# The first weight block of a seven-product pair behind plain or down columns is split one column sooner

## Chip, core and metric

The kernel runs on one core of one Trainium2 chip. The metric is the device time of one execution in microseconds (us). Engines are called as the profile calls them: PE multiplies matrices (PEld is its weight load), DVE, ACT and POOL work on elements, SP issues most DMAs.

## What is computed

One layer of a decoder, for a prompt of 512 tokens and for 32 sample tokens (8 sequences of 4) with the same weights; the kernel holds all 544 tokens side by side. Cut to what matters here:

```python
D_MODEL = 1024
D_FF = 2816

def _swiglu(x, w_gate, w_up, w_down):
    return (jax.nn.silu(x @ w_gate) * (x @ w_up)) @ w_down

def _layer(x, pos, p, attn_cache, ml_state):
    x = x + 0.5 * _swiglu(_rmsnorm(x, p['ffn1_norm']), p['ffn1_w_gate'], p['ffn1_w_up'], p['ffn1_w_down'])
    h = _rmsnorm(x, p['mix_norm'])
    ...
    x = x + mix @ p['w_out']
    x = x + 0.5 * _swiglu(_rmsnorm(x, p['ffn2_norm']), p['ffn2_w_gate'], p['ffn2_w_up'], p['ffn2_w_down'])
```

Between the two lines, `h` is projected by `w_in`, and dilated attention and mLSTM heads make `mix` from it. Everything is float32. The two SwiGLU blocks (ffn1 and ffn2) are the parts that the change touches.

## The kernel before

**Split operands.** A float32 product is made of three faster ones. Each operand is split into a high part (a rounded copy, made on ACT) and a low part (what is left, a subtraction on DVE). PE then adds high x high, high x low, low x high. For the weights the parts are the tiles `whi` and `wlo`. Both come, like the temporary `ws`, from one rotation of eight buffers (tag `wsp`): a new tile takes the buffer of the one eight before it and waits until that one has been read.

**Columns.** PE works column by column, one column being 128 columns of a weight matrix. `run` gets a list of jobs. A plain `Job` is one column: 8 blocks of 128 rows, each with 3 products for 2 halves of the tokens, 48 matmuls. A down column (a `Job` on `w_down`) is of the same kind; its result is added to the residual `xT[m]` by one DVE instruction, `x<-mm,x`. In the first plain columns of a block the gate and up results also pass through DVE and ACT (`zg`, `zu`, `hh`, `hl`), and `FastNorm.operands` prepares the sums of activation blocks that the pairs need (`xn`, `xd`, split into `oh` and `ol`).

**Seven-product pairs.** A `Fast` job computes two gate and two up columns together, as a product of 2x2 blocks with seven block products where the plain way has eight. The activation sides of the seven are `b11`, `t1`, `t2`, `b22`, `t3`, `b21` and `t4`, all prepared before. Each of the seven steps is 24 matmuls. Its weight side is made by `Fast.split(n)`:

- step 0: the raw block `a11`, split;
- step 1: `ws = a21 + a22`, split; step 2: `ws = ws - a11`, split; step 3: `ws = a12 - ws`, split (one tile, overwritten each time);
- step 4: `a21 = a11 - a21` in the raw tile (`wraw<-wraw` in the profile), split; steps 5 and 6: `a12` and `a22`, split.

So steps 1 to 4 cost two DVE instructions and one on ACT. The products accumulate in PSUM: steps 0, 2, 4 and 6 in one bank pair (`a`), steps 1 and 3 in two smaller ones (`c`, `aux` in the profile), step 5 in another. After steps 0, 1 and 2 ACT copies the bank as it stands (`p1`, `p5`, `p6`, all `p` in the profile): the next step into the same bank may start only after its copy.

**Raw blocks.** The raw tiles (`wraw`) have three buffers. The loader starts the DMAs of a raw tile when the one three before it is used up; for a pair that is at step 4 for the upper half (`top`) and step 6 for the lower (`low`).

**What sets the order.** The order of instructions on each engine is fixed while the program is built. `Order` keeps a clock for each engine and a list of threads (generators). A thread yields a time, and maybe a condition, at which it may go on. `poll` lets threads go on whose time has come by PE's clock; it is called after each block of rows (6 matmuls in a column, 3 in a pair). Threads with a lower priority number go first. `cost` holds the planned durations: on DVE 0.15 us + 1.05 ns for each element of a row, on ACT for a copy 0.18 us + 0.75 ns, on PE one matmul of 272 in 272 / 2180 us. A thread that waits for a result yields mostly the planned end + 0.2 - 0.3 us. These times decide only which instruction is written first; on the chip each engine takes its instructions in the order written and waits for semaphores.

**The splitter.** In `run`, one thread goes through the jobs in order and writes the splits. `pos[n]` is the place of job n in units, a plain job counting 2 and a pair 7, and `unit[0]` is where PE is: it is set when a column begins and grows by one with each step of a pair. A plain job is split when PE has reached `pos[n] - 4` (`pos[n] - 3` behind a pair). Step s of a pair is split when PE has reached `pos[n] + s - 2`, step 1 at `pos[n] - 2`.

A block of 2816 hidden columns is done in three parts (8, 8 and 6 blocks of 128). In each half the first part has 8 plain columns, 2 pairs and 8 down columns; the second 4 pairs and 8 down columns; the third 3 pairs and 8 down columns. So there are six places at which a pair follows a plain or a down column: one behind plain and two behind down columns in each half. Between the halves lies the mixing stage (attention and mLSTM), in which all engines work.

Of the kernel before, what the change touches and what calls it, by code (L numbers as in the profile page):

```python
# [52 lines left out]
class Order:  # L53
# [89 lines left out]
    def R(self, *aps):  # L143
        return max(self.ready.get(a.tensor.name, (0.0, ""))[0] for a in aps) + 0.2

    def U(self, *aps):
        return max(self.used.get(a.tensor.name, (0.0, ""))[0] for a in aps) + 0.2
# [100 lines left out]
def hybrid_layer_kernel(ctx: ExitStack, tc: tile.TileContext, I: dict, C: dict, O: list):  # L248
# [20 lines left out]
    def aux():  # L269
        return pax.tile([P, 512], F32, name="aux", tag="aux")  # L270
# [16 lines left out]
    def mm(out, lhsT, rhs, start=True, stop=True, beside=False, **kw):  # L287
        nc.tensor.matmul(out, lhsT, rhs, start=start, stop=stop, **kw)  # L288
        n = size(rhs)
        od.issue("pe", 0.05 if beside else n / (2180.0 if rhs.dtype == F32R else 595.0), [out], [lhsT, rhs],  # L290
                 False, (part(lhsT.shape[0]), part(size(lhsT))))
# [314 lines left out]
    at, unit, used = [0], [0], [0]  # L606

    def run(jobs):
        raws = []
        pos, n = [], 0  # L610
        for j in jobs:
            for r in (j.top, j.low) if isinstance(j, Fast) else (j.raw,):
                if r not in raws:
                    raws.append(r)
            pos.append(n)
            n += 7 if isinstance(j, Fast) else 2

        def loader():
            for n, r in enumerate(raws):
                if n >= 3:  # L620
                    old = raws[n - 3]
                    yield 0, 0, lambda: old.left == 0
                    yield U(old.t)
                if r.t is None:
                    r.load()
            yield 0

        def splitter():
            for n, j in enumerate(jobs):
                if isinstance(j, Fast):  # L630
                    for s in range(7):
                        raw = j.low if s else j.top
                        yield 0, 0, lambda: unit[0] >= pos[n] + s - (3 if s == 1 else 2) and raw.t is not None
                        yield from j.split(s)
                else:
                    ahead = 3 if n and isinstance(jobs[n - 1], Fast) else 4
                    yield 0, 0, lambda: unit[0] >= pos[n] - ahead and j.raw.t is not None
                    yield R(j.raw.t) - 0.3
                    yield from j.split()

        od.spawn(loader(), 0)
        od.spawn(splitter(), 1)
        od.poll()

        def slot():
            od.need(lambda: od.avail("mm", 1))
            od.take("mm", 1)
            ps = pmm.tile([P, 2, 512], F32, name="mm", tag="mm")
            od.poll()
            return ps  # L650

        def products(j, ps, ks, hs=(0, 1)):
            od.need(lambda: j.w is not None)
            hi, lo = j.w
            for k in ks:
                od.need(lambda: j.xs(k) is not None)
                xh, xl = j.xs(k)
                for a, (w, x) in enumerate(((hi, xh), (hi, xl), (lo, xh))):
                    for h in hs:
                        mm(ps[:, h, :HN], w[:, k, :], x[:, h * HN:(h + 1) * HN],  # L660
                           start=j.start and k == 0 and a == 0, stop=j.stop and k == j.nk - 1 and a == 2)
                od.poll()

        def finish(j, ps):
            if j.stop:
                od.spawn(j.after(ps[:, :, :HN], ps), 0)
                od.poll()

        kept = [None]

        def fast(j, more):
            bank = {"a": kept[0] or slot()}
            for n, (name, b) in enumerate(j.steps):
                unit[0] += n > 0
                od.need(lambda: j.w[n] is not None)
                hi, lo = j.w[n]
                if n == 1:
                    od.need(lambda: sum(f <= od.t for f in od.free["aux"]) >= 2)
                    od.take("aux", 2)
                    bank["c"] = aux(), aux()  # L680
                elif n == 5:
                    bank["b"] = slot()
                for i in range(2):
                    ps = bank[b][i] if b == "c" else bank[b][:, i]
                    for k in range(4):
                        od.need(lambda: j.op(name, k) is not None)
                        xh, xl = j.op(name, k)
                        for a, (w, x) in enumerate(((hi, xh), (hi, xl), (lo, xh))):
                            mm(ps[:, :HN], w[:, 4 * i + k, :], x, start=n in (0, 1, 5) and k == 0 and a == 0,
                               stop=k == 3 and a == 2, skip_group_check=True)  # L690
                        od.poll()
                od.spawn(j.post(n, bank, more), 0)
                od.poll()
            kept[0] = bank["b"] if more else None

        first = [(j, slot()) for j in jobs[:2]]
        for ks in (range(0, 4), range(4, 8)):
            for i, (j, ps) in enumerate(first):
                for k in ks:
                    products(j, ps, (k,))  # L700
                    used[0] = max(used[0], k + 1)
                    od.poll()
                if 7 in ks:
                    finish(j, ps)
                    at[0], unit[0] = i + 1, pos[i + 1]
        for i, j in enumerate(jobs[2:]):
            at[0], unit[0] = i + 2, pos[i + 2]
            if isinstance(j, Fast):
                fast(j, isinstance(jobs[i + 3], Fast))
                continue  # L710
            if j.start:
                ps = slot()
            if j is jobs[-1]:
                for h in range(2):
                    products(j, ps, range(j.nk), (h,))
                    od.spawn(last_half(h, ps[:, h, :HN]), 0)
                    od.poll()
                continue
            products(j, ps, range(j.nk))
            finish(j, ps)  # L720
# [133 lines left out]
    jobs = ffn_jobs("ffn1", lambda: n1, n2.add)  # L854
# [976 lines left out]
    def last_half(h, ps):  # L1831
        m = KD - 1
        x = xT[m]
        h_ = slice(h * HN, (h + 1) * HN)
        dve.scalar_tensor_tensor(x[:, h_], ps, 0.5, x[:, h_], op0=OP.mult, op1=OP.add)
        yield R(x), 1
        p = aux()
        yt = t2("yt", (P, 2, P))
        if h:
            yst = t2("yst", (NS, P))  # L1840
            tr(p[0:NS, 2 * P:3 * P], x[:, S:N], ident)
        for b in range(2):
            c = (2 * h + b) * P
            tr(p[:, b * P:(b + 1) * P], x[:, c:c + P], ident)
        if h:
            dve.tensor_copy(yst, p[0:NS, 2 * P:3 * P])
        act.copy(yt.rearrange("p b d -> p (b d)"), p[:, 0:2 * P])
        done(p)
        yield R(yt) - 0.3
        if h:  # L1850
            dma.dma_start(ysm[:, m * P:(m + 1) * P], yst)
        dma.dma_start(yp[:, 2 * h:2 * h + 2, m * P:(m + 1) * P], yt)
# [96 lines left out]
```

## Time and profile before

| | us |
|---|---|
| median of 3 runs | 1116.19 |
| lowest, highest | 1116.14, 1116.45 |
| profiled execution | 1116.02 |
| its span, first to last instruction | 1114.2 |

The profile is of one execution. Times in it count from the span's start. A row of the timeline gives the start, the duration, the engine, the line of the kernel (226 and 288 are lines of helpers that write all element work and all matmuls), the operation, output<-inputs, shapes and, in brackets, how long the engine was idle before it and for whom. Matmuls are drawn with a modelled length (0.29 us for 272 columns), although the next one starts 0.125 us after: their starts count, not their ends. A row of the waits gives who waited for whom, the total in us, how often, and the longest. A row of the stretches gives the length, then busy time and count of PE, PEld, DVE, ACT and POOL, the granted clock, the DMA engines' share and GB/s.

### The profile page before, as it was taken

To read this page: it belongs to the slowest core of one execution; us is meant where nothing else is said; L and a number is where in the kernel's file an instruction comes from. 1 tells how busy PE (TensorE), PEld (TensorE's weight loads), DVE (VectorE), ACT (ScalarE), POOL (GpSimd) and SP (SyncE) were. 2 spreads that over 40 slices of the span, in tenths; PEclk is the share of its full clock that TensorE was granted. 3 is DMA by queue.
4 is the path that set the end of the run, shared out by engine and by line. 5 is a ranking of instruction groups with operands and counts; after the bars stand their busy time and mean duration, and the time that the engine had idled before them with its cause. 6 is when DMAs were issued, how large, how long until landed. Compare 5 with 4: busy or idle time off the path is not lost.

```text
span 1114.2 us, 21328 instructions
## 1 busy us (share of the span) xinstructions
PE 1095.4 (98%) x8807; PEld 1043.7 (94%) x8807; DVE 750.6 (67%) x1178; ACT 507.9 (46%) x926; POOL 94.1 (8%) x104
## 2 busy tenths in 40 slices
PE   7999999999999999999999999999999999999998
PEld 5999999999999999998887977999999999999997
DVE  5888338873487779678776746688862788537852
ACT  5545215551255455466744544453541355314541
POOL 0000000000000000174444310000000000000000
PEclk9999999999999999999999999999999999999999
DMA  7214412342134547684987494341242222422232
GB/s 234 79 39 132 126 48 77 111 155 76 39 95 132 169 148 168 192 247 125 308 271 252 158 320 155 104 131 56 76 151 76 77 76 76 152 77 76 67 108 58
DMA packets 143404, 145.36 MB, mean 130 GB/s; under 512 B 9028, under 2 KB 120964, under 8 KB 143308
## 3 DMA queue, kind: packets, MB, share of 16 engines
q1 hardware_dynamic: 143244, 144.01, 41.8%
q8 instruction: 69, 1.13, 0.4%
q14 instruction: 27, 0.22, 0.1%
q0 software_dynamic: 64, 0.00, 0.0%
HBM read 132.57 MB, written 9.18 MB: 127 GB/s over the span
## 4 chain that ended last, share of the span: by engine, by line
PE 89%; DVE 6%; ACT 2%; issue 1%; DMA 1%; SPq 0%; DVEq 0%; ACTq 0%
PE mm L288 73%; PE aux L288 13%; PE aux L294 4%; DVE wlo L226 2%; ACT whi L226 2%; DVE ws L226 1%; DVE wraw L226 1%; DMA wraw<-in_ffn_w_up_dram 1%; DMA xt<-in_x_prompt_dram 0%; DVE zu L226 0%; DVE ol L226 0%; ACT p L226 0%; DVE xd L226 0%; SPq L226 0%; DVE hl L226 0%
## 5 line engine op out<-in xcount | busy, mean ns | idle before, releaser
L226 ACT CAST whi<-wraw 128x1024 fp32r<-128x1024 f32 (+3 forms) x180 | 174.2, 988 | 130.5 <-PE mm L288 97.2
L226 DVE TENSOR_TENSOR wlo<-wraw,whi 128x1024 fp32r<-128x1024 f32 (+3 forms) x180 | 208.2, 1165 | 22.8 <-ACT whi L226 22.7
L288 PE MATMUL mm<-oh,wlo 128*128 128x272 f32 x720 | 209.6, 291 | 2.1 <-DVE wlo L226 2.0
L288 PE MATMUL mm<-oh,whi 128*128 128x272 f32 x720 | 207.5, 288 | 0.0
L288 PE MATMUL mm<-ol,whi 128*128 128x272 f32 x720 | 207.2, 288 | 0.0
L288 PE MATMUL mm<-xh,whi 128*128 128x272 f32 x704 | 153.7, 300 | 0.2 <-ACT whi L226 0.2
L288 PE MATMUL mm<-hh,whi 128*128 128x272 f32 x704 | 147.3, 289 | 0.5 <-DVE x L226 0.5
L288 PE MATMUL mm<-xl,whi 128*128 128x272 f32 x704 | 146.0, 289 | 0.5 <-DVE xl L226 0.5
L288 PE MATMUL mm<-hl,whi 128*128 128x272 f32 x704 | 146.5, 288 | 0.0
L288 PE MATMUL mm<-hh,wlo 128*128 128x272 f32 x704 | 146.4, 288 | 0.0
L288 PE MATMUL mm<-xh,wlo 128*128 128x272 f32 x704 | 146.0, 289 | 0.3 <-DVE wlo L226 0.3
L288 PEld LDWEIGHTS mm<-oh,wlo 128*128 128x128 f32 x720 | 135.5, 188 | 5.4 <-DVE wlo L226 4.4
L226 DVE SCALAR_TENSOR_TENSOR x<-mm,x 128x544 f32<-128x544 f32 (+1 forms) x49 | 34.9, 713 | 154.9 <-PE mm L288 154.9
L288 PEld LDWEIGHTS mm<-oh,whi 128*128 128x128 f32 x720 | 135.6, 188 | 0.0
L288 PEld LDWEIGHTS mm<-ol,whi 128*128 128x128 f32 x720 | 135.5, 188 | 0.0
L288 PEld LDWEIGHTS mm<-xh,whi 128*128 128x128 f32 x704 | 109.8, 189 | 12.3 <-issue 11.6
L288 PEld LDWEIGHTS mm<-hh,whi 128*128 128x128 f32 x704 | 110.8, 188 | 0.9 <-DVE x L226 0.7
L288 PEld LDWEIGHTS mm<-xl,whi 128*128 128x128 f32 x704 | 110.7, 189 | 0.8 <-DVE xl L226 0.8
L288 PEld LDWEIGHTS mm<-xh,wlo 128*128 128x128 f32 x704 | 110.8, 189 | 0.6 <-DVE wlo L226 0.6
L288 PEld LDWEIGHTS mm<-hh,wlo 128*128 128x128 f32 x704 | 110.9, 188 | 0.0
L288 PEld LDWEIGHTS mm<-hl,whi 128*128 128x128 f32 x704 | 110.7, 188 | 0.0
L226 ACT CAST whi<-ws 128x1024 fp32r<-128x1024 f32 x54 | 56.7, 1051 | 105.9 <-DVE ws L226 105.9
(328 smaller groups left out, 1755.6 us busy)
## 6 DMA issues: line engine op xcount, KB each, us to landing
wraw<-in_ffn_w_gate_dram SPq DMA_DIRECT2D x40, 512.0 KB
wraw<-in_ffn_w_up_dram SPq DMA_DIRECT2D x36, 512.0 KB
wraw<-in_ffn_w_down_dram SPq DMA_DIRECT2D x16, 1024.0 KB
kv<-in_cache_k_win_dram SPq DMA_DIRECT2D x56, 256.0 KB
kv<-in_cache_v_win_dram SPq DMA_DIRECT2D x56, 256.0 KB
wraw<-in_w_in_dram SPq DMA_DIRECT2D x16, 512.0 KB
wraw<-in_ffn_w_down_dram SPq DMA_DIRECT2D x8, 768.0 KB
wraw<-in_w_in_dram SPq DMA_DIRECT2D x6, 1024.0 KB
```

Source lines behind the costliest of these rows:

```text
L226: r = fn(*args, **kw)
L288: nc.tensor.matmul(out, lhsT, rhs, start=start, stop=stop, **kw)
L294: nc.tensor.transpose(out, in_, idn)
```

## The change

```diff
         def splitter():
             for n, j in enumerate(jobs):
                 if isinstance(j, Fast):
+                    first = 2 if isinstance(jobs[n - 1], Fast) else 4
                     for s in range(7):
                         raw = j.low if s else j.top
-                        yield 0, 0, lambda: unit[0] >= pos[n] + s - (3 if s == 1 else 2) and raw.t is not None
+                        yield 0, 0, lambda: unit[0] >= pos[n] + s - (first, 3, 2)[min(s, 2)] and raw.t is not None
                         yield from j.split(s)
```

For a pair whose predecessor is a plain or down column, step 0 may be split when PE has reached `pos[n] - 4`, the start of the column two before the pair, where it was `pos[n] - 2`, the start of the column just before. For a pair behind a pair nothing changes, nor for steps 1 to 6 of any pair: their conditions read as before.

## Prediction

> **What bounds the kernel now.** I read the page first: the shares of busy time, the granted clock, and the chain of work that ended last.
>
> ```profile
> span 1114.2 us, 21328 instructions
> PE 1095.4 (98%) x8807; PEld 1043.7 (94%) x8807; DVE 750.6 (67%) x1178; ACT 507.9 (46%) x926; POOL 94.1 (8%) x104
> ...
> PEclk9999999999999999999999999999999999999999
> ...
> PE 89%; DVE 6%; ACT 2%; issue 1%; DMA 1%; SPq 0%; DVEq 0%; ACTq 0%
> ```
>
> PE is busy almost throughout, at the full clock, so the change can only give back time in which PE stands still. The DVE and ACT parts of the chain say where: they lie at the six places where a run of seven-product pairs begins. I name them G1 (66 to 85 us), G2 (158 to 177), G3 (295 to 311), G4 (774 to 791), G5 (871 to 883) and G6 (1005 to 1017). G1 and G4 follow plain columns, the other four follow down columns. Next, the view of the waits with PE's rows alone, once around each place. First G1, then G2, then G3 (around G5 and G6 it answers the same two numbers), then G4's longer one (its other row is 0.2 again).
>
> ```profile
> PE mm L288 <- DVE wlo L226: 1.1, 2, 0.9
> PE aux L288 <- DVE wlo L226: 0.4, 1, 0.4
> ```
> ```profile
> PE aux L288 <- DVE wlo L226: 0.3, 1, 0.3
> PE mm L288 <- DVE wlo L226: 0.2, 1, 0.2
> ```
> ```profile
> PE aux L288 <- DVE wlo L226: 0.2, 1, 0.2
> PE mm L288 <- DVE wlo L226: 0.2, 1, 0.2
> ```
> ```profile
> PE aux L288 <- DVE wlo L226: 1.0, 1, 1.0
> ```
>
> PE waits for low parts of weight blocks: 13 times, 4.4 us idle. A stop costs more than its idle figure. The timeline at G2's first stop shows it (start, duration, engine):
>
> ```profile
> 171.91 0.29 PE L288 MATMUL aux<-oh,whi 128*128 128x272 f32 x1
> 171.92 0.19 PEld L288 LDWEIGHTS aux<-ol,whi 128*128 128x128 f32 x1
> 172.04 0.29 PE L288 MATMUL aux<-ol,whi 128*128 128x272 f32 x1
> ...
> 172.59 0.39 PE L288 MATMUL aux<-oh,wlo 128*128 128x272 f32 x1 [0.26 <-DVE wlo L226]
> ...
> 172.81 0.29 PE L288 MATMUL aux<-oh,whi 128*128 128x272 f32 x1
> ```
>
> Matmuls that don't wait start 0.125 us apart. The one that waits starts 0.55 after its predecessor, 0.42 late where the idle figure says 0.26 (it counts from the end of the drawn 0.29 us), and the next starts 0.22 later instead of 0.125. So a stop costs its idle figure + 0.165 + 0.1, about 0.27 more. By place: G2 0.3 + 0.2 + 0.54 = 1.0; G3, G5 and G6 0.4 + 0.54 = 0.94 each; G1 1.5 + 0.81 = 2.3; G4 1.2 + 0.54 + about 0.2 (a short one that the wait view doesn't list) = 1.9. **All stops together: 8.0 us, 0.7%.** That is the most that the change can win.
>
> **Part 1: what moves.** The diff alters one number. A pair's step 0 may be split when the column two before it begins, not the one before. Two instructions per place move in the order in which the program writes them: `whi` (ACT) and `wlo` (DVE) of step 0. No instruction is added or removed, no DMA or tile added; the rotation of the eight `wsp` buffers is the same, since the splitter is one sequential generator. SP's queue is passed by nothing: a raw block is freed by steps 4 and 6. POOL has no instruction at these places. ACT has run ahead already: in G2 step 0's `whi` runs as soon as its buffer is free.
>
> ```profile
> 144.79 1.05 ACT L226 CAST whi<-wraw 128x1024 fp32r<-128x1024 f32 x1 [4.99 <-PE mm L288]
> ```
>
> So on the chip only `wlo` moves directly, from behind one residual update `x` to before it. DVE in G2 (first row from the window just before):
>
> ```profile
> 151.03 0.73 DVE L226 SCALAR_TENSOR_TENSOR x<-mm,x 128x544 f32<-128x544 f32 x1 [4.13 <-PE mm L288]
> ```
> ```profile
> 157.69 1.22 DVE L226 TENSOR_TENSOR wlo<-wraw,whi 128x1024 fp32r<-128x1024 f32 x1
> 158.83 1.22 DVE L226 TENSOR_TENSOR ws<-wraw 128x1024 f32<-128x1024 f32 x1
> 161.22 1.22 DVE L226 TENSOR_TENSOR wlo<-ws,whi 128x1024 fp32r<-128x1024 f32 x1 [1.17 <-ACT whi L226]
> 163.11 0.72 DVE L226 SCALAR_TENSOR_TENSOR x<-mm,x 128x544 f32<-128x544 f32 x1 [0.67 <-PE mm L288]
> 163.75 1.22 DVE L226 TENSOR_TENSOR ws<-ws,wraw 128x1024 f32<-128x1024 f32 x1
> ```
>
> `wlo` of step 0 goes from 157.69 to about 151.7, where DVE is idle; that costs nothing, and by itself it also wins nothing here, since step 2's `ws` stays at 163.75 behind the last `x`. The gain has to come through ACT's order.
>
> **Part 2: ACT's order in G2, G3, G5, G6.**
>
> ```profile
> 166.11 0.62 ACT L226 COPY p<-mm 128x544 f32<-128x544 f32 x1 [4.93 <-PE mm L288]
> 166.62 1.05 ACT L226 CAST whi<-ws 128x1024 fp32r<-128x1024 f32 x1
> 167.62 0.39 ACT L226 COPY p<-aux 128x272 f32<-128x272 f32 x1
> 169.12 0.39 ACT L226 COPY p<-aux 128x272 f32<-128x272 f32 x1 [1.12 <-PE aux L288]
> 170.23 1.05 ACT L226 CAST whi<-ws 128x1024 fp32r<-128x1024 f32 x1 [0.72 <-DVE ws L226]
> 172.12 0.61 ACT L226 COPY p<-mm 128x544 f32<-128x544 f32 x1 [0.84 <-PE mm L288]
> 173.70 2.95 ACT L226 CAST whi<-wraw 128x1024 fp32r<-128x1024 f32 x3 [0.98 <-DVE wraw L226]
> ```
>
> Step 2's `whi` had its input at 163.75 + 1.22 = 164.97 but ran at 166.62, because the copy `p` of step 0's product stands before it on ACT and waits for PE. From there DVE and ACT hand the work to each other, 3.6 us a step (1.22 `ws`, 1.05 `whi`, 1.22 `wlo`, hand-overs), while PE takes 3.0; steps 3 and 4 come late.
>
> Which of `p` and `whi` is written first the planner decides, by the durations in its `cost`. I use them for the order alone; all times below are the trace's. Counted from the pair's start, before: step 1's `wlo` is written at the very end of the last column, so DVE is planned busy to 1.2 with it, to 1.95 with `x`, to 3.2 with step 2's `ws`; `whi` is due 0.1 earlier, at 3.1, and the product ends at 2.99, so `p` is first, by a tenth. After: step 0's `wlo` has left the last column, step 1's `ws` starts 1.2 earlier there and its `wlo` is planned done before the pair starts. Then `x` to 0.92, `ws` to 2.15, `whi` due at 2.05 against 2.99. **It goes ahead of `p`**, by more than two of the planner's polls (0.37 apart). Going on by the same rules, step 3's `whi` is due at 5.84 against 5.99 for the two copies of step 1: also ahead, but narrowly.
>
> On the chip this gives in G2: `whi` 165.0 to 166.05, in front of a `p` that can't start before 166.11; `wlo` to 167.3; step 3's `ws` to 168.6, `whi` to 169.65, `wlo` to 170.9, needed at 172.17: this stop goes. The copies of step 1 end at about 170.4 instead of 169.5; the next writer of their bank is step 3, at 171.9. Then `wraw` to 172.1, `p` 172.12 to 172.73 (now the late one), `whi` of step 4 to 173.7, `wlo` to 174.97, needed at 171.92 + 3.0 + 0.25 = 175.17: this stop goes too, by 0.2. **Saved: 1.0 + 3 x 0.94 = 3.8 us.** If step 3's `whi` is written behind the copies, it starts at 169.5, step 4's `wlo` ends near 175.35, 0.2 late, and with its 0.1 restart each of four places gives back 0.3.
>
> **Part 3: G1 and G4.** Here DVE itself is full (a row from its timeline, then the stretch from 64 to 82: DVE's busy time is the third figure).
>
> ```profile
> 63.97 0.72 DVE L226 TENSOR_TENSOR zu<-mm,rb 128x544 f32<-128x544 f32 x1 [1.75 <-PE mm L288]
> ```
> ```profile
> 64.00:82.00 18.00, 16.76 (x132) 16.32 (x131) 17.77 (x22) 8.22 (x13) 0.00 (x0) 1.00 0.00 1
> ```
>
> In G1 DVE works without a break from 64 to 82 and idles 1.75 us just before. One `wlo`, 1.22 drawn and 1.14 in sequence, moves into that idle time, and all behind it comes about 1.2 earlier: of the 2.3 us of stops I take **1.2**. The operand splits (`ol`, `xn`) that it is put before slip by 1.1 into the same gap; their products come twenty microseconds later. In G4 the same move is cut short by ACT:
>
> ```profile
> 779.91 0.61 ACT L226 COPY p<-mm 128x544 f32<-128x544 f32 x1 [3.06 <-PE mm L288]
> 780.42 1.06 ACT L226 CAST whi<-ws 128x1024 fp32r<-128x1024 f32 x1
> ```
>
> By the planner's durations `p` stays ahead of `whi` here (due 3.2 after the start against 2.99), so `whi` still ends at 781.48, `wlo` can start at 781.5 instead of 781.85, and **0.4** is won. Bounds: nothing, or all 1.9 if the two swap.
>
> **Sum:** 3.8 + 1.2 + 0.4 = 5.4 us. The profiled execution took 1116.02 us (span 1114.2, 1.8 around it): 1110.6. The median before is 1116.19, 0.17 above it, so the forecast is **1110.8 us**.
>
> [...]
>
> **Rivals.**
> 1. *Step 3's `whi` stays behind the copies* (planned margin 0.15): 4 x 0.3 given back, 1112.0. Chance 0.12.
> 2. *ACT's order in the four down places stays*: then only G1 and G4 gain, 1.6 us, 1114.6. For it speaks that before the two were a tenth apart, so an error in my counting matters; against it that a whole `wlo` leaves DVE's plan. Chance 0.14.
> 3. *The change does nothing*: `wlo` was never late at step 0 (158.9 against a need at 163.2), and the later chain doesn't move. 1116.2, chance 0.05.
> 4. *Slower*: the planner's clock shifts, and with it the laying out of the mixing stage between the two halves, where all engines and the DMA queues meet.
>
> ```profile
> 399.00:694.00 295.00, 293.70 (x2530) 252.22 (x2529) 212.50 (x479) 159.79 (x412) 93.23 (x96) 1.00 0.71 217
> ```
>
> PE is idle there for only 1.3 us. If ties between its many threads fell otherwise and PE had to wait for late attention data, each wait like the present one costs 1.3; from the sixth (7.8 against 5.4 won) the kernel is slower, 1118.6. Against it: eight down columns in front let every planned queue run empty, so that the stage starts from the same relative state. Chance 0.05.
>
> **Numbers.** Forecast, 1109.2 to 1112.2 (bounds of G1 and G4, and small stops at step 4): 0.60. Rivals as above. A further 0.04 for nearly all 8.0 saved, 1108.2 to 1109.2. A measurement of this kernel tells about 0.2%, 2.2 us, from no change: below 1114.0 counts as faster. Faster: 0.60 + 0.12 + 0.04 = 0.76. Same: 0.14 + 0.05 = 0.19. Slower: 0.05. The range 1109.2 to 1115.0 leaves out the slower case, no change and the best one: 0.14.
>
> **What would show it.** In G2, G3, G5 and G6 the cast `whi<-ws` of step 2 starts right behind its `ws`, before the `p` copy, and PE's waits for `wlo` are gone. In G1 the wait count falls from three to two and DVE's full stretch is a block shorter; in G4 the long wait shrinks from 1.0 to about 0.6. The forecast is wrong if `p` still precedes `whi` in the down places, if stops appear at later pairs, or if the mixing stage gets longer than 295 us.

## The result and the profile after

| | before | after |
|---|---|---|
| median of the runs taken together, us | 1116.32 (1116.14 to 1119.60) | 1110.69 (1109.69 to 1111.60) |
| profiled execution, us | 1116.02 | 1111.60 |
| its span, us | 1114.2 | 1109.8 |

The ratio is 0.9947, with a 95% interval of 0.9930 to 0.9964: 5.6 us faster. The forecast was 1110.8.

The page of the changed kernel; the lines are the span, the busy times, and the chain of work that ended last by engine.

```profile
span 1109.8 us, 21330 instructions
...
PE 1092.7 (98%) x8807; PEld 1043.0 (94%) x8807; DVE 748.2 (67%) x1178; ACT 508.3 (46%) x926; POOL 93.8 (8%) x104
...
PE 90%; DVE 5%; DMA 2%; ACT 2%; issue 1%; SPq 0%; DVEq 0%; ACTq 0%
```

The same 8807 matmuls, the same work on DVE and ACT, one point less of the chain on DVE. PE's waits in the changed kernel, first around G1 (60 to 100 us), then around G4 (770 to 815):

```profile
PE aux L288 <- DVE wlo L226: 0.3, 1, 0.3
PE mm L288 <- DVE wlo L226: 0.2, 1, 0.2
```
```profile
PE aux L288 <- DVE wlo L226: 0.9, 1, 0.9
PE mm L288 <- DVE wlo L226: 0.2, 1, 0.2
```

Around G2, G3, G5 and G6 this view lists nothing at all. G1 has lost its longest stop (0.9), G4's long one has shrunk by only a tenth. How G2 got rid of its stops stands in ACT's timeline (start, duration, idle time before and what ended it):

```profile
163.73 1.05 ACT L226 CAST whi<-ws 128x1024 fp32r<-128x1024 f32 x1 [4.97 <-DVE ws L226]
164.78 0.61 ACT L226 COPY p<-mm 128x544 f32<-128x544 f32 x1
167.32 1.05 ACT L226 CAST whi<-ws 128x1024 fp32r<-128x1024 f32 x1 [1.93 <-DVE ws L226]
168.28 0.67 ACT L226 COPY p<-aux 128x272 f32<-128x272 f32 x2
170.79 0.61 ACT L226 COPY p<-mm 128x544 f32<-128x544 f32 x1 [1.84 <-PE mm L288]
171.30 1.05 ACT L226 CAST whi<-wraw 128x1024 fp32r<-128x1024 f32 x1
```

Before, `p` stood first at 166.11 and step 2's `whi` at 166.62. Now step 2's `whi` is first, and step 3's too stands ahead of the two copies of step 1. DVE follows it:

```profile
162.42 1.22 DVE L226 TENSOR_TENSOR ws<-ws,wraw 128x1024 f32<-128x1024 f32 x1
164.81 1.22 DVE L226 TENSOR_TENSOR wlo<-ws,whi 128x1024 fp32r<-128x1024 f32 x1 [1.17 <-ACT whi L226]
166.07 1.22 DVE L226 TENSOR_TENSOR ws<-wraw,ws 128x1024 f32<-128x1024 f32 x1
168.41 1.22 DVE L226 TENSOR_TENSOR wlo<-ws,whi 128x1024 fp32r<-128x1024 f32 x1 [1.12 <-ACT whi L226]
169.55 1.22 DVE L226 TENSOR_TENSOR wraw<-wraw 128x1024 f32<-128x1024 f32 x1
172.38 2.36 DVE L226 TENSOR_TENSOR wlo<-wraw,whi 128x1024 fp32r<-128x1024 f32 x2 [1.61 <-ACT whi L226]
```

Step 2's `ws` ends at 163.64 and its `whi` starts 0.09 later; before, 166.62 came 1.65 after the end of `ws`. Ahead of step 4's `wlo` DVE now stands idle for 1.61 us until ACT's `whi` is there: its own work is no longer what holds that step.

**Time by place.** Whole times can't tell terms of a few tenths, since the executions of one program on one chip differ by 0.6 us (e12) to 5.1 us (e6). So I set the starts of the matmuls of two traces side by side, first to last, and took the change of the lag over each place. PE does them in the same order in all runs, but for one small matmul near 130 us in e6, e9 and e10. The table has all runs against the first profile of before, in us; minus is shorter. "Start" is the stretch before G1, "attention" the mixing stage, and "six" the sum of G1 to G6. Two new stops of e6, told below, lie behind G1 and G4 and count in "all" alone.

```
                 start    G1     G2     G3     G4     G5     G6     six  attention  all
before again     -1.07  -0.01   0.00   0.00   0.00   0.01   0.00    0.0   -0.07   -0.64
after            -0.01  -1.20  -0.98  -0.92  -0.35  -1.00  -0.94   -5.4    0.93   -4.27
after again      -0.77  -1.21  -0.98  -0.92  -0.36  -1.00  -0.94   -5.4    0.43   -5.63
e1 down only     -0.83  -0.01  -0.99  -0.92   0.00  -1.00  -0.96   -3.9    1.90   -2.60
e2 plain only    -0.15  -1.20   0.01  -0.01  -0.32   0.00   0.02   -1.5   -0.07   -1.73
e3                0.76  -0.01  -0.81  -0.81   0.01  -0.83  -0.79   -3.2    0.65   -1.99
e4                2.15  -1.20   0.01  -0.02  -0.32   0.00   0.01   -1.5    0.01    0.43
e5               -2.40  -1.27  -0.98  -0.92  -1.25  -1.00  -0.94   -6.4   -0.01   -8.77
e5 again         -0.82  -1.26  -0.98  -0.92  -1.25  -1.00  -0.94   -6.4    0.00   -6.81
e6               -0.54  -2.09  -0.96  -0.95  -1.84  -1.01  -0.94   -7.8    1.61    0.63
e9                1.25  -2.09  -0.93  -0.95  -1.81  -0.94  -0.95   -7.7    0.52   -5.70
e10              -0.25  -2.02  -0.96  -0.94  -1.80  -0.97  -0.97   -7.7    1.48   -6.62
e10 again        -0.39  -2.03  -0.96  -0.94  -1.80  -0.97  -0.97   -7.7    1.70   -5.99
```

Between the two executions of one program the six places repeat to 0.01 us; the start (up to 1.58 apart) and the attention stage (up to 0.50) do not. The change took 5.4 us out of the six places.

### The profile page after: what moved, and what is told of

The parts are those of the page before. It is cut to its first block, busy times and chain, and to the rows that moved or that the text cites. A ratio compares the mean times of both kernels' runs of the same rounds, so it can differ in the third digit from the quotient of the medians.

```text
span 1109.8 us, 21330 instructions
## 1 busy us (share of the span) xinstructions
PE 1092.7 (98%) x8807; PEld 1043.0 (94%) x8807; DVE 748.2 (67%) x1178; ACT 508.3 (46%) x926; POOL 93.8 (8%) x104
## 4 chain that ended last, share of the span: by engine, by line
PE 90%; DVE 5%; DMA 2%; ACT 2%; issue 1%; SPq 0%; DVEq 0%; ACTq 0%
PE mm L288 73%; PE aux L288 14%; PE aux L294 4%; DVE wlo L226 2%; ACT whi L226 1%; DMA wraw<-in_ffn_w_up_dram 1%; DVE ws L226 1%; DVE wraw L226 1%; DMA xt<-in_x_prompt_dram 1%; DVE ol L226 0%; DVE zu L226 0%; SPq L226 0%; DVE hl L226 0%; DVE xd L226 0%; ACT p L226 0%
```

## The experiments

**Theories.** Mine: at the four down places the gain comes from ACT's order alone (step 2's `whi` ahead of `p`), at G1 from relief of a full DVE, and at G4 the same relief is cut short by `p` on ACT. Rival A: the earlier split by itself does it, and ACT's new order only goes along. Rival B: part of the 5 us is chance between executions.

**e1 and e2: the change in parts.** The condition is narrowed to columns on `w_down` (e1) or to the others (e2):

```diff
-                    first = 2 if isinstance(jobs[n - 1], Fast) else 4
+                    first = 4 if not isinstance(jobs[n - 1], Fast) and jobs[n - 1].raw.w.shape[0] == FF else 2   # e1
+                    first = 4 if not isinstance(jobs[n - 1], Fast) and jobs[n - 1].raw.w.shape[0] == D else 2    # e2
```

> Step 0 is split one column sooner only at the four places behind down columns (G2, G3, G5, G6); behind plain columns (G1, G4) as before. Theory (each place gains by itself, the down places through ACT's order): 3.8 us less than before, 0.9 to 1.0 at each of the four places and nothing at G1 and G4, so near 1112.4. Rival (the places hang together through the planner's clock, or the gain is mostly DVE's relief behind plain columns): clearly less than 3 us gained, or the gain of a place differs from that in the changed kernel.

> Step 0 is split one column sooner only at the two places behind plain columns (G1, G4). Theory (DVE is full there and one low-part subtraction of 1.14 us leaves its full stretch): 1.2 us gained at G1, 0.3 at G4, nothing elsewhere, so 1.5 us less than before, near 1114.7. Rival (ACT's order matters there too, or the places hang together): more than 2 us, or a change at the down places.

e1: 1113.38 against 1115.68 for the kernel before on the same chip, ratio 0.9979 (0.9970 to 0.9988). e2: 1114.10, 0.9987 (0.9978 to 0.9996). By place they add up: 3.9 + 1.5 = 5.4, each place as in the whole change. e1's whole time came out above its share: in its profile the attention stage was 1.9 us longer, with PE at half clock for 3.4 us of it (granted 0.65 from 682 to 684 us and 0.50 from 684 to 686; see the last section).

**e3 and e4: ACT's order apart from the split.** e3 is the kernel before, with the first copy of a pair behind down columns held until step 2's `whi` is written; the split stays where it was. e4 is the changed kernel with the opposite hold.

```diff
 # e3, on the kernel before
+        def held(j, n, bank, more):
+            if n == 0 and j.down:
+                yield 0, 0, lambda: j.hi2      # set when step 2's whi is written
+            yield from j.post(n, bank, more)
 # e4, in Fast.split of the changed kernel
+            if n == 2 and self.down:
+                yield 0, 0, lambda: self.p1    # set when step 0's copy is written
             act.copy(hi, src)
```

> The kernel before, with step 0's split left where it was; only ACT's copy of step 0's product is written behind step 2's high part, at the four down places. Nothing on DVE, PE or the DMA queues changes its order. Theory (the gain there is this swap on ACT and nothing else): the first stop (step 3) goes, 0.4 + 0.1 us at each place; step 3's high part still stands behind the two copies of step 1, so step 4 stays about 0.2 late; 0.7 gained at each place, 2.8 in all, near 1113.5. Rival (the gain comes from step 0's block being split sooner): nothing gained, 1116.3.

> The changed kernel, step 0 split one column sooner at all six places, but at the four down places step 2's high part may be written only behind the copy of step 0's product, as it stood before. Theory (the swap on ACT carries the gain of the down places): both stops come back there, about 0.95 a place; G1 and G4 keep their 1.5 us, so near 1114.8. Rival (the earlier split by itself carries it): nothing is lost against the changed kernel, near 1110.7.

e3: 1113.55, ratio 0.9982 (0.9973 to 0.9991). e4: 1115.53, 0.9996 (0.9987 to 1.0005). By place e3 wins 0.79 to 0.83 at each down place without moving the split (0.7 was expected), and e4 wins 0.02 or less there with the split moved. Rival A falls. That rests on the places: e4 keeps 1.5 us at G1 and G4, but its whole time can't be told from before's; in its profile the start was 2.2 us longer. ACT's timeline of e3 in G2:

```profile
165.80 1.05 ACT L226 CAST whi<-ws 128x1024 fp32r<-128x1024 f32 x1 [3.88 <-DVE ws L226]
166.85 0.62 ACT L226 COPY p<-mm 128x544 f32<-128x544 f32 x1
168.35 0.39 ACT L226 COPY p<-aux 128x272 f32<-128x272 f32 x1 [0.89 <-PE aux L288]
169.86 0.39 ACT L226 COPY p<-aux 128x272 f32<-128x272 f32 x1 [1.12 <-PE aux L288]
170.14 1.05 ACT L226 CAST whi<-ws 128x1024 fp32r<-128x1024 f32 x1
```

Here step 3's `whi` stays behind both copies: this is the case of rival 1 of the prediction. Against the change, e3 wins 0.11 to 0.17 less a place, where 0.3 was the price. And e4's in the same place, with PE's waits:

```profile
166.87 0.61 ACT L226 COPY p<-mm 128x544 f32<-128x544 f32 x1 [6.03 <-PE mm L288]
167.38 1.05 ACT L226 CAST whi<-ws 128x1024 fp32r<-128x1024 f32 x1
```
```profile
PE aux L288 <- DVE wlo L226: 0.3, 1, 0.3
PE mm L288 <- DVE wlo L226: 0.2, 1, 0.2
```

ACT sits idle for 6 us in front of a copy that waits for PE. For the last 1.1 of them the input of the cast behind it is there (DVE ends that `ws` at 165.73), and the cast doesn't go ahead. The two waits of before are back.

**e7 and e8: the two kernels once more,** with no edit, for rival B.

> The changed kernel once more. In its first profile the mixing stage took 0.9 us longer than before, with one new wait of PE there for a transposed operand. If that is chance of one execution, the stage differs from before by less than 0.2 us in this one, or by another stop at another place, and the six places gain the same to 0.1. If the stage really takes back part of the gain (PE comes sooner to data that do not), the same stop of about 0.9 is there again.

> The kernel before once more, to see how far one execution of the same program differs from another by stages: the six places should agree to 0.05 us; the start and the mixing stage, where data come by DMA, may differ by up to 1 us.

e7: 1111.32, ratio 0.9957 (0.9945 to 0.9968). e8: 1116.40, 1.0001 (0.9993 to 1.0010). The kernel before against itself comes out equal, the changed one again 0.4% below, and the six places gain 5.4 once more: for the places rival B falls. For the whole time it doesn't quite: against its own runs of before (1115.96) e7 is 4.6 us faster, where the first comparison gave 5.6. The attention stage of the changed kernel was longer in both its profiles, by 0.93 and 0.43, nearly all at one transpose of cached keys near 538 us of before's time. For this stop the view of PE's waits names ACT in the first profile and a DMA in e7:

```profile
PE aux L294 <- ACT vs L226: 0.7, 1, 0.7
```
```profile
PE aux L294 <- DMA kv<-in_cache_k_win_dram: 0.3, 1, 0.3
```

So the stop came again at the same place, as the second reading had it, but at half the size. e5, which contains the whole change, did not have it in either of its profiles, so it isn't a fixed price of the change. What holds PE there, and why in one execution and not in the other, stays open.

**e5: the same swap at G1 and G4.** The changed kernel, with the hold of e3 for pairs behind plain columns:

```diff
+            if n == 0 and j.plain:
+                yield 0, 0, lambda: j.hi2
```

> The changed kernel, and at the two plain places (G1, G4) ACT's copy of step 0's product is written behind step 2's high part too. Theory (in G4 ACT's order still holds step 2 up, in G1 DVE alone does): G4's long stop falls from 1.1 us to about 0.1, the next one stays near 0.4, so 1.0 is gained there; nothing at G1; 1.0 less than the changed kernel. Rival (DVE's load is what holds both): nothing gained at either.

1108.04, ratio 0.9931 (0.9919 to 0.9943), beside e7 on the same chip (0.9945 to 0.9968): faster than the changed kernel there. G4 wins 1.25 where the change wins 0.35; G1 stays. ACT in G4 of the changed kernel, then of e5:

```profile
778.10 0.61 ACT L226 COPY p<-mm 128x544 f32<-128x544 f32 x1 [4.31 <-PE mm L288]
778.61 1.05 ACT L226 CAST whi<-ws 128x1024 fp32r<-128x1024 f32 x1
```
```profile
773.36 1.05 ACT L226 CAST whi<-ws 128x1024 fp32r<-128x1024 f32 x1 [3.28 <-DVE ws L226]
774.41 0.61 ACT L226 COPY p<-mm 128x544 f32<-128x544 f32 x1
```

The long wait of 0.9 leaves PE's list; the 0.2 stays. In G1 the swap wins only 0.07. DVE in G1 of the changed kernel shows why:

```profile
73.88 0.72 DVE L226 TENSOR_TENSOR xd<-xn,xd 128x544 f32<-128x544 f32 x1
74.57 1.23 DVE L226 TENSOR_TENSOR wlo<-ws,whi 128x1024 fp32r<-128x1024 f32 x1
```

DVE itself was busy with an activation sum until `wlo` began, so an earlier `whi` doesn't help. e5 bears it out: there `whi` ends at 71.34, and `wlo` still starts at 72.08, right behind the same sum.

**e6, e9 and e10: relief for DVE.** In G1 and G4, DVE also prepares the activation side `t4`, which PE needs only at step 6, the last of the seven: two `xd` and two `ol`, 2.5 us in all (4 x 0.63 in sequence). On top of e5, these are held until the pair has reached step 4 (e6), step 3 (e9) or step 2 (e10):

```diff
+            yield 0, 0, lambda: unit[0] >= marks[self.due] + 4     # 3 in e9, 2 in e10
             for j in range(2):                                     # the t4 sums
```

> As the run with the copy behind at the plain places, and the last pair of activation operands (t4, four DVE instructions of 0.64 us in sequence) is made only from step 4 on, out of the stretch in which DVE is full. Theory (DVE's load is the rest of the stops at G1 and G4): 0.8 gained at G1 and 1.4 at G4 against the changed kernel, 2.2 in all, if the four don't make a later step late. Rival (they only move the wait): a new stop at step 5 or 6 of these two pairs, or at the pair behind, takes back 1 us or more.

> e5 with the four instructions on the mean's row (t4) held back on DVE by three steps in the two places behind plain columns, where e6 held them by four. Theory: in e6 the stretch of the second to fourth step gained 0.9 us in the first half and 0.6 us more than e5's in the second, and all of it was lost to a 3.0 us stop at the seventh step, because the four came too late for the sums there; one step sooner they are in time, the stop is gone, and the gain of the stretch stays: 2.0 us in the first half and 1.7 us in the second against the kernel before, 1.2 us less than e5 in all: about 1106.8. Rival: the four stand again in front of the blocks of the fourth step or later, which then come late: the time is e5's 1108.0 or above. A stop of over 1 us at the seventh step would say that three steps are still too late.

> As the run with three steps, with two. Theory: in time for the sums too, but the four instructions (2.6 us of DVE or so) now fall ahead of the blocks of the third and fourth step, so part of the stops of 0.2 to 1.2 us there comes back: 1107.2 to 1108.0, between the run with three steps and e5. Rival: what counts is only that the second step's block goes ahead of them: same time as the run with three steps, about 1106.8.

e6: 1116.68, ratio 1.0006 (0.9997 to 1.0016); the rival held, all that it won and more was lost. The wait view of e6 has the same single row around G1 and around G4:

```profile
PE mm L288 <- DVE ol L226: 2.8, 1, 2.8
```

The stretch itself gained 2.1 and 1.8 us, but the sums missed their own step, and half clock behind the second stop (granted 0.50 from 800 to 802 us) cost more (see the last section). e9: 1109.73, 0.9934 (0.9918 to 0.9949); e10: 1109.16, 0.9935 (0.9922 to 0.9948). Both keep the gain of the stretch, and PE's wait view lists nothing at all in G1 and G4. DVE in G1 of e10:

```profile
72.93 1.23 DVE L226 TENSOR_TENSOR wlo<-ws,whi 128x1024 fp32r<-128x1024 f32 x1 [0.54 <-ACT whi L226]
74.19 1.22 DVE L226 TENSOR_TENSOR ws<-wraw,ws 128x1024 f32<-128x1024 f32 x1
75.33 0.72 DVE L226 TENSOR_TENSOR hl<-zu,hh 128x544 fp32r<-128x544 f32 x1
75.96 0.72 DVE L226 TENSOR_TENSOR xd<-xn,xd 128x544 f32<-128x544 f32 x1
77.05 1.22 DVE L226 TENSOR_TENSOR wlo<-ws,whi 128x1024 fp32r<-128x1024 f32 x1 [0.36 <-ACT whi L226]
```

Two idle gaps where before DVE had none. By place, the rival of the two expectations for e10 held: two steps do as well as three (7.7 and 7.7), since what counts is that step 2's block no longer stands behind them. The times expected for e9 and e10, 1106.8 and up to 1108.0, were missed: the whole times did not show the 1.3 us that both have over e5 by place.

**e11 and e12: e5 and e10 again, on one chip.**

> The kernel of e5 once more, unchanged, on one chip with the kernel of e10, since their times came out alike (ratios 0.9931 and 0.9935) although e10's six places are 1.3 us shorter in the profiles. If the rest was chance in the stretch before the first product, which has varied from 2.4 us shorter to 2.2 us longer between executions, the six places are again about 6.4 us shorter than before's, and the time is 1109 to 1110, 6.4 below before's.

> The kernel of e10 once more. If the gain of the stretch (2.0 and 1.8 us in the two places behind plain columns) reaches the end, its time is about 1.3 us below e5's in the same call, about 1108. Rival: something outside the six places gives it back (the attention stage, 1.5 us longer in e10's profile, or the start), and the two are alike again: then that stretch is longer by about as much in this profile too.

e5: 1109.57, ratio 0.9942 (0.9928 to 0.9956). e10: 1109.81, 0.9942 (0.9930 to 0.9955). The six places repeat (6.4 and 7.7), and so does e10's longer attention stage: 1.70, after 1.48. The rival held for the two profiled executions: what e10 wins in the places it gave back there. Granted clock of e10 (the figure ahead of the last two), then of e10 again, then of e5 again in the same stage:

```profile
670.00:672.00 2.00, 1.82 (x9) 1.82 (x10) 0.93 (x3) 1.84 (x9) 0.00 (x0) 0.64 0.15 46
672.00:674.00 2.00, 2.00 (x11) 0.40 (x9) 0.47 (x2) 0.62 (x3) 0.00 (x0) 0.51 0.24 41
```
```profile
680.00:682.00 2.00, 2.00 (x15) 2.00 (x14) 1.89 (x11) 1.03 (x3) 1.18 (x2) 0.68 0.00 0
682.00:684.00 2.00, 2.00 (x10) 1.75 (x11) 1.56 (x5) 0.00 (x0) 0.00 (x0) 0.50 0.43 131
```
```profile
670.00:672.00 2.00, 0.95 (x7) 0.95 (x8) 1.08 (x4) 1.94 (x9) 0.00 (x0) 1.00 0.05 15
672.00:674.00 2.00, 2.00 (x17) 1.01 (x16) 1.13 (x3) 1.37 (x7) 0.00 (x0) 1.00 0.04 12
```

For some 3.4 us PE ran at half clock in both profiles of e10. But this doesn't explain the whole times. The mean granted clock is on record for every run, and one such stretch lowers it by 0.0015 (half of 3.413 us in 1107.5), so that a mean of 0.999 leaves no room for one. It is 0.998 in six of the ten runs of e10's kernel and never below 0.999 in the twelve of e5's; yet e10's four runs at 0.999 or above took 1108.59 to 1110.36, no less than its six at 0.998 (1108.17 to 1109.95). So whether e10 beats e5 stays open, and also what takes back its gain in the runs without a profile. e5 beats the kernel before; that it beats the changed one is shown by whole time on one chip alone, since its second ratio (0.9928 to 0.9956) overlaps that of e7, and by place in both profiles, by 1.0.

## Why the prediction was right

**The bound.** Right: by place, all of the gain lay in PE's stops for `wlo`, and the price of a stop (idle figure + 0.27) held. Where both stops of a down place went, 0.92 to 1.00 came back, against 0.94 and 1.0 in the sum.

**Part 2, ACT's order.** Right, step for step. Step 2's `whi` is ahead of `p` in all four places; step 3's is ahead of the copies, the narrow case. 3.84 us came of it, 3.8 was forecast. e3 and e4 show the mechanism: with the order alone 0.8 a place, without it nothing. That ACT kept to the written order here is seen in e4: it stood idle for 6.03 us in front of a copy, though the cast behind it had its input for the last 1.1 of them.

**Part 3.** G1 was 1.20 (forecast 1.2): the stop of 0.9 went, the next shrank by 0.1. DVE is no longer full between 64 and 82 us in this row of the changed kernel (the third busy time; 17.77 before):

```profile
64.00:82.00 18.00, 17.71 (x141) 17.49 (x140) 16.85 (x22) 9.31 (x15) 0.00 (x0) 1.00 0.00 1
```

G4 was 0.35 (forecast 0.4): `p` did stay ahead of `whi`, and `wlo` started 0.03 us after `whi` ended. Only the split between the stops was off: the long one was to shrink to 0.6 and shrank to 0.9, and the short one, which the wait view doesn't list, went instead.

**Rivals.** Rival 1 did not come; by e3 it would have cost about half of its price. Rivals 2 and 3 are out: e4 brings rival 2 about, and gives by place what rival 2 said, 1.5 against 1.6 us. Rival 4's mechanism, another order of the work in the mixing stage, did not occur: the order of PE, SP, POOL and ACT in that stage is the same in both kernels. But that stage did take 0.4 to 0.9 us longer in the two profiles of the change, which the sum had at nothing. That is one of the signs that the prediction named for its being wrong (the stage longer than 295 us). It came without the rival's mechanism, smaller than its price of 1.3 a wait, and not in e5.

**The sum** of 5.4 was met by the places to a tenth. That the median fell within 0.1 us of the forecast is luck: with the longer mixing stage the places leave 4.5 to 5.0 us, e7 measured 4.6, and the start alone varies by 4.5 us between executions.

## What to carry to other kernels

Where one engine serves two chains in a fixed order, look for an instruction that waits on a third engine with a ready one behind it: the time is in their order (0.79 to 0.83 us a place in e3), and a small edit upstream can flip it. When a change is a fraction of a per cent, line up two traces instruction by instruction; here the gains by place repeated to 0.01 us where the whole times of one program on one chip scattered by 0.6 to 5.1 us. Work that is needed late (the sums for step 6) may move behind work that is needed sooner, but only by as much as its own due time allows: held until step 2 or 3, the sums left PE no wait at these places; held until step 4, they stopped it for 2.8 us.

## What was not expected of the hardware

**Half clock without a long stop.** In e1, in e6 and in both profiles of e10 PE ran at half clock for some 3.4 us in the attention stage (granted clock 0.50 or 0.51 in one row of 2 us of each), which was 1.5 to 1.9 us longer there; in e10, matmuls stood 0.227 apart instead of 0.125 from 670.73 on, and full spacing was back at 674.4. The only long stop near it took 1.56 us from start to start (before 670.18). This stop doesn't decide it: before and e5 again have the same 1.56 us there at full clock, and in e1 and in e10 again the clock fell only 10 us behind it. e6's two stops of 3.1 us ended differently: after the second the clock fell, after the first it stayed. Rows of e6 (clock ahead of the last two figures):

```profile
88.00:92.00 4.00, 1.19 (x9) 0.98 (x8) 3.57 (x6) 1.39 (x4) 0.00 (x0) 1.00 0.49 151
92.00:96.00 4.00, 4.00 (x34) 4.00 (x33) 3.35 (x4) 1.88 (x3) 0.00 (x0) 1.00 0.02 4
...
800.00:802.00 2.00, 2.00 (x11) 2.00 (x10) 2.00 (x3) 0.16 (x1) 0.00 (x0) 0.50 0.00 0
```

The lengths are regular in the clock records of the traces: each half-clock stretch ahead of the kernel's end lasts 3.413 us, and the full-clock stretches up to a change are whole multiples of it (with 3.4133, 651.95 us in e10 is 191 times it, 1092.27 in the first profile of before 320 times and 1088.85 in that of the change 319 times). What sets the clock down, no run here shows: it fell behind one stop of 3.1 us and not behind the other, and with one of 1.56 us nearby in some executions and not in others.

**The start.** The stretch before the first pair varied by 4.5 us between executions; of the 1.96 us between the two profiles of e5 it is 1.58. In e4, 18 matmuls are in the stretch from 18 to 22 us where e5 again has 33, first e4's rows, then those of e5 again:

```profile
18.00:20.00 2.00, 2.00 (x8) 1.43 (x8) 1.53 (x3) 1.07 (x3) 0.00 (x0) 1.00 1.08 348
20.00:22.00 2.00, 2.00 (x10) 2.00 (x10) 2.00 (x6) 1.47 (x4) 0.00 (x0) 1.00 0.56 103
```
```profile
18.00:20.00 2.00, 2.00 (x17) 1.79 (x16) 2.00 (x5) 1.82 (x5) 0.00 (x0) 1.00 1.08 344
20.00:22.00 2.00, 2.00 (x16) 1.58 (x15) 1.97 (x7) 1.64 (x4) 0.00 (x0) 1.00 0.87 238
```

The granted clock reads 1.00 in both, though most of e4's matmuls stand 0.21 to 0.27 us apart there (those of 272 columns 0.227, as at half clock). The traces say why: their first clock record, at full clock, begins at 23.53 us in e4 and at 17.39 in e5 again, and the view prints 1.00 where there is no record. Over the executions it begins between 11.99 us (the first profile of e5, with the shortest start) and 23.53 (e4, with the longest). The first profile of before shows both sides of it: matmuls of 272 columns stand 0.227 us apart up to 16.6 us and 0.125 from 19.6 on, and its first record begins at 19.32. So in these profiles a clock of 1.00 ahead of the first record says nothing of the speed; the spacing of equal matmuls does.
